# A fourth pair of k-tiles by seven block products in five of the eight chunks of an up projection

## The chip, the core and the metric

The kernel runs on one core of a Trainium2 chip. The core has a tensor engine (PE: matmuls and transposes, with a separate lane PEld that loads weights), a vector engine (DVE), a scalar engine (ACT), a general engine (POOL, here almost only an issuer of transfers) and a synchronisation engine (SP, which issues most transfers). Each takes its instructions in order from a queue of its own; they meet at semaphores. The metric is the device time of one execution in microseconds (us). Before the change it is 1054.91 us, the median of 3 runs (1053.62 to 1054.93).

## The reference, cut to what matters

One decoder layer in float32 on 256 positions of width 2048. Only the last part is touched:

```python
h = _rmsnorm(x, norm_mlp_pre)               # (256, 2048)
u = jnp.square(jax.nn.relu(h @ w_up))       # w_up is (2048, 8192)
x = x + _rmsnorm(u @ w_down, norm_mlp_post)
```

## The kernel before

**Precision.** Each float32 operand is split into a `hi` part, rounded to the format of the matmul, and a `lo` part, what is left. ACT makes `hi` with a copy, DVE makes `lo` with a subtraction (`split`, L288 to L292). A product is then three matmuls into the same bank: hi by hi, hi by lo, lo by hi (`three`). Where a weight row carries the gain of the norm, both engines apply it on the way (`split_gain`, L294 to L297; the DVE instruction is then a SCALAR_TENSOR_TENSOR).

**Tiles of the up projection.** The 8192 columns are cut into eight chunks of 1024 (`j`, 0 to 7), the 2048 rows into sixteen k-tiles of 128. The activations lie transposed in `hT` as hi and lo. A plain k-tile step ("k") loads one 128 x 1024 piece of `w_up` into a raw buffer through SP's queue, splits it, and runs 2 blocks of positions x 2 halves of columns x 3 = 12 matmuls of 512 columns into four accumulators.

**Seven products.** A step "w" takes two k-tiles together as a 2 x 2 by 2 x 2 block product and makes it from seven block products instead of eight. On the weights, DVE makes three sums (L343, L347, L348: two tiles `t` and `u`), and four tiles are split: the first block `b11` of 512 columns and the second row `b` from the buffer `ab`, then `u` and `t`. On the activations four "left sums" are made once per pair (`left_sums`) and kept in `st`; the pair's k-tiles of `hT` are overwritten with gain applied. Of the seven products three go to the accumulators and four to banks `m`; at the end of the chunk `close` combines the `m` into `c` on ACT and DVE, and four adds of DVE (L880) bring them to the accumulators. Seven times three are 21 matmuls. Before the change, chunks 1 to 7 have three such pairs (k-tiles 0 to 5) and ten plain k-tiles, in the order k-tiles 6 to 10, pair 0, 11, 12, pair 1, 13, pair 2, 14, 15 (`UP_STEPS`). Both k-tiles of a pair go through POOL's queue into one buffer `ab` of 2048 columns; in chunk 7 pairs 1 and 2 use two raw buffers instead.

**End of a chunk.** For each of its four accumulators (`up_evac`): the add on DVE, relu with the norm's scale on ACT (`r`, L883), four 128 x 128 transposes on PE (`rt`, L285) into the same bank, and the square on ACT into `uT` (L895). That work stands among the next chunk's first k-tiles. The bank is then free, and the next chunk's `m` are put into these four banks.

**What sets the order.** Every queue's order is written out by the program itself. `Weights` holds the list of tile splits and emits them `W_AHEAD` = 6 tiles ahead of the matmul that is being emitted; eight `hi` and eight `lo` buffers go round, so a split may run on the chip when PE is done with the tile eight before it. Sums of a pair are emitted two tiles ahead of its first split, but not before the end of the pair in front. `Flow` keeps a clock of its own, fed with a fixed cost per matmul, and inserts the evacuation chains when their delays have passed; `finish` forces what is left of a chain to be emitted at once. Raw buffers are five (`RAW_BUFS`).

## Time and profile before

| | before |
|---|---|
| three timed runs, median | 1054.91 us |
| profiled execution, its own time | 1055.26 us |
| span of the profiled execution, first to last instruction | 1053.5 us |
| PE busy in the span | 1042.6 us, 99% |
| DVE busy in the span | 819.8 us, 78% |
| ACT busy in the span | 622.5 us, 59% |
| mean granted clock of the tensor engine | 0.997 |

How to read it: "busy" is the time in which an engine worked on at least one instruction, as a share of the span. Lines of a timeline give the start in us from the span's start, the duration, engine, source line, operation, what it writes and reads, and in brackets the idle time of the engine ahead of it with what ended that. Matmuls overlap in the pipeline: the duration shown is that of one, while the distance between starts is what a row of them costs. In the windows, "(x200)" is a count of instructions, and PEclk the granted clock as a share of full speed. The first transposes of chunks 2 to 7 start at 451.38, 494.78, 538.18, 581.58, 624.98 and 668.38 us; "first transpose" always means the set of four 128 x 128 transposes of the first accumulator.

### The profile page before, as it was taken

The page shows a single profiled execution, that of the slowest core. Times are in us where ns is not written, and L with a number is a line of the kernel's source. Part 1 is how long each engine was busy: PE and PEld are TensorE (multiplying, and loading weights), DVE is VectorE, ACT ScalarE, POOL GpSimd, SP SyncE. Part 2 cuts the span into 40 slices and gives each one's busy share as a digit, 9 for nine tenths or more (in the row PEclk, how much of TensorE's full clock was granted, in tenths as well). Part 3 has the DMA queues.
Part 4 walks back from the last instruction along what each step waited for, and adds up shares of the span by engine and source line. Part 5 has one row for each costly group of instructions (what it writes and reads, how often), then busy time and mean ns, then how long its engine had stood idle before and what let it go on. Part 6 is the DMA issues. An engine that isn't in the chain of part 4 may idle for free.

```text
span 1053.5 us, 13402 instructions
## 1 busy us (share of the span) xinstructions
PE 1042.6 (99%) x4863; PEld 869.2 (83%) x4863; DVE 819.8 (78%) x1090; ACT 622.5 (59%) x832; POOL 46.7 (4%) x88
## 2 busy tenths in 40 slices
PE   9999999999999999999999999999999999999996
PEld 6888889888888788888888888888888888888885
DVE  6676536567557679879888888887899988998985
ACT  6584536565545467666665666666566665666661
POOL 0000000000000000010000100000000000000000
PEclk9999999999999999999999999999999999999998
DMA  9975447454447295647656466467466564667732
GB/s 299 355 236 145 144 130 241 143 161 158 141 167 234 79 350 167 222 143 237 197 186 201 160 215 207 148 224 238 162 218 206 195 221 148 224 210 253 262 121 80
DMA packets 74306, 206.26 MB, mean 196 GB/s; under 512 B 6912, under 2 KB 11520, under 8 KB 73856
## 3 DMA queue, kind: packets, MB, share of 16 engines
q1 hardware_dynamic: 63584, 168.06, 49.0%
q0 software_dynamic: 10080, 36.70, 9.7%
q8 instruction: 38, 0.62, 0.2%
q10 hardware_dynamic: 576, 0.64, 0.2%
q14 instruction: 28, 0.23, 0.1%
HBM read 201.18 MB, written 4.19 MB: 195 GB/s over the span
## 4 chain that ended last, share of the span: by engine, by line
PE 97%; DVE 1%; issue 1%; DMA 0%; ACT 0%; POOL 0%; DVEq 0%; POOLq 0%; ACTq 0%
PE y L281 27%; PE acc_u L281 25%; PE acc_o L281 8%; PE m L281 5%; PE md L281 4%; PE acc_qk L281 4%; PE acc_v L281 4%; PE acc_ckv L281 2%; PE acc_ukv L281 2%; PE acc_q L281 2%; PE acc_cq L281 2%; PE acc_k L281 2%; PE acc_uq L281 2%; PE rt L285 1%; PE sc_b L281 1%
## 5 line engine op out<-in xcount | busy, mean ns | idle before, releaser
L292 DVE TENSOR_TENSOR lo<-raw,hi 128x1024 fp32r<-128x1024 f32 (+3 forms) x219 | 249.2, 1153 | 93.8 <-ACT hi L291 93.1
L291 ACT ACTIVATE hi<-raw 128x1024 fp32r<-128x1024 f32 (+3 forms) x219 | 215.9, 1001 | 117.1 <-PE y L281 40.0
L281 PE MATMUL y<-hi,uhi 128*128 128x512 f32 x394 | 153.6, 390 | 0.0
L281 PE MATMUL y<-hi,ulo 128*128 128x512 f32 x394 | 153.3, 389 | 0.0
L281 PE MATMUL y<-lo,uhi 128*128 128x512 f32 x394 | 153.3, 389 | 0.0
L281 PE MATMUL acc_u<-hi,hT_hi 128*128 128x512 f32 x386 | 153.2, 397 | 0.0
L281 PE MATMUL acc_u<-hi,hT_lo 128*128 128x512 f32 x386 | 150.9, 391 | 0.4 <-DVE hT_lo L292 0.4
L281 PE MATMUL acc_u<-lo,hT_hi 128*128 128x512 f32 x386 | 150.6, 390 | 0.0
L296 DVE SCALAR_TENSOR_TENSOR lo<-raw,gcol,hi 128x1024 fp32r<-128x1024 f32 x86 | 107.6, 1278 | 12.5 <-ACT hi L295 12.3
L295 ACT ACTIVATE hi<-raw,gcol 128x1024 fp32r<-128x1024 f32 x86 | 97.9, 1151 | 24.2 <-PE acc_u L281 13.6
L281 PEld LDWEIGHTS y<-hi,uhi 128*128 128x128 f32 x394 | 74.0, 188 | 15.3
L281 PEld LDWEIGHTS y<-lo,uhi 128*128 128x128 f32 x394 | 74.0, 188 | 15.3
L281 PEld LDWEIGHTS y<-hi,ulo 128*128 128x128 f32 x394 | 73.9, 188 | 15.3
L281 PEld LDWEIGHTS acc_u<-hi,hT_lo 128*128 128x128 f32 x386 | 72.4, 188 | 16.2 <-DVE hT_lo L292 0.8
L281 PEld LDWEIGHTS acc_u<-lo,hT_hi 128*128 128x128 f32 x386 | 72.6, 188 | 14.2
L281 PEld LDWEIGHTS acc_u<-hi,hT_hi 128*128 128x128 f32 x386 | 72.6, 188 | 14.0
L281 PE MATMUL acc_o<-hi,mixT_hi 128*128 128x512 f32 x128 | 51.8, 405 | 0.0
L281 PE MATMUL acc_o<-hi,mixT_lo 128*128 128x512 f32 x128 | 50.2, 392 | 0.0
L281 PE MATMUL acc_o<-lo,mixT_hi 128*128 128x512 f32 x128 | 50.0, 390 | 0.0
L291 ACT ACTIVATE hi<-ab 128x512 fp32r<-128x512 f32 (+1 forms) x38 | 32.0, 843 | 30.0 <-PE acc_u L281 23.2
L281 PE MATMUL m<-hi,st 128*128 128x512 f32 x126 | 45.6, 389 | 0.0
L292 DVE TENSOR_TENSOR lo<-st_down,hi 128x1024 fp32r<-128x1024 f32 x34 | 40.9, 1218 | 2.7 <-ACT hi L291 2.7
(309 smaller groups left out, 1947.7 us busy)
## 6 DMA issues: line engine op xcount, KB each, us to landing
raw<-in_w_down SPq DMA_DIRECT2D x94, 512.0 KB, 4.7
raw<-in_w_up SPq DMA_DIRECT2D x86, 512.0 KB, 4.5
raw<-in_w_in SPq DMA_DIRECT2D x55, 512.0 KB, 5.0
ab<-in_w_up POOLq DMA_DIRECT2D x36, 512.0 KB, 4.9
ab_down<-in_w_down POOLq DMA_DIRECT2D x34, 512.0 KB, 6.2
raw<-in_w_out SPq DMA_DIRECT2D x32, 512.0 KB, 4.0
raw<-in_w_in SPq DMA_DIRECT2D x16, 288.0 KB, 2.8
raw<-in_w_ukv SPq DMA_DIRECT2D x8, 512.0 KB, 4.8
```

Of the source, the lines that this page charges most:

```text
L281: nc.tensor.matmul(out, a, b, start=start, stop=stop)
L285: nc.tensor.transpose(out, a, ident)
L291: nc.scalar.activation(hi, src, AF.Copy)
L292: nc.vector.tensor_tensor(out=lo, in0=src, in1=hi.bitcast(F32), op=OP.subtract)
L295: nc.scalar.activation(hi, src, AF.Copy, scale=g)
L296: nc.vector.scalar_tensor_tensor(out=lo, in0=src, scalar=g, in1=hi.bitcast(F32), op0=OP.mult, op1=OP.subtract)
```

## The change

Chunks 2 to 6 get a fourth pair (k-tiles 6 and 7), so they have four pairs and eight plain k-tiles, in the order k-tiles 8 to 11, pair 0, 12, pair 1, 13, pair 2, 14, pair 3, 15. Chunks 1 and 7 stay at three pairs. The fourth left sums are made during chunk 1, once its k-tiles 6 and 7 have been used plainly. From chunk 2 on, k-tiles 6 and 7 of `hT` carry the gain, so chunk 7 loads them without it. A second buffer `ab2` is used in turn with `ab`, and pair 2 of chunk 6 goes through two raw buffers. To make room, `st` keeps only three of the four left sums for pairs 0 to 2; the fourth (s1) is written into the block of `hT` that the seven products don't read; and two of the `uT` tiles lie in `ab2`. In a chunk with four pairs the last pair runs its products into `m` ahead of the others. Before the first pair of a chunk the evacuation chains of the previous one are finished.

```diff
-N_SEVEN, SUMS_AHEAD = 3, 2
-UP_STEPS = [("k", k) for k in range(6, 11)]
-for _i, _n in enumerate(((11, 12), (13,), (14, 15))):
-    UP_STEPS += [("w", _i)] + [("k", k) for k in _n]
+SUMS_AHEAD = 2
+
+
+UP_PAIRS = [()] + [("ab", "ab2", "ab", "ab2")] * 5 + [("ab2", "ab", "raw", "ab"), ("ab", "raw", "raw")]
+
+
+def up_steps(first, *groups):
+    steps = [("k", k) for k in first]
+    for i, ks in enumerate(groups):
+        steps += [("w", i)] + [("k", k) for k in ks]
+    return steps
+
+
+THREE = up_steps(range(6, 11), (11, 12), (13,), (14, 15))
+FOUR = up_steps(range(8, 12), (12,), (13,), (14,), (15,))
+UP_STEPS = [up_steps(range(16)), THREE] + [FOUR] * 5 + [THREE]
+
+ST = 13 * 256
+N_SEVEN = [sum(w == "w" for w, _ in steps) for steps in UP_STEPS]
...
-            if j == FF // CW - 1 and kp:
+            if UP_PAIRS[j][kp] == "raw":
                 return [weights.load(up_weight(j, 2 * kp + i), CW, f"raw_w{j}_{kp}{i}") for i in range(2)]
-            return load_two(late["ab"], nc.gpsimd if (j, kp) > (1, 0) else nc.sync,
+            return load_two(late[UP_PAIRS[j][kp]], nc.gpsimd if (j, kp) > (1, 0) else nc.sync,
...
-        for what, k in [("k", k) for k in range(KD)] if j == 0 else UP_STEPS:
+        for what, k in UP_STEPS[j]:
             if what == "k":
-                ts = [weights.plan(up_weight(j, k), 1, CW, gcol[:, 8 + k:9 + k])]
+
+                ts = [weights.plan(up_weight(j, k), 1, CW, *([gcol[:, 8 + k:9 + k]] if j < 2 or k >= 2 * max(N_SEVEN) else []))]
...
-            if j in (12, 13):
-                t2 = late["ab"][:, (j - 12) * CW:(j - 11) * CW]
+            if j in (10, 11, 12, 13):
+                t2 = late["ab2" if j < 12 else "ab"][:, j % 2 * CW:(j % 2 + 1) * CW]
...
-        four_sums(q, f)
-        st = [late["st"][:, i * 512:(i + 1) * 512] for i in (2 * kp, 2 * kp + 1)]
+        fs, qs = [x.rearrange("p (k s) -> p k s", s=P) for x in (f, q)]
+        keep = kp >= min(N_SEVEN[1:])
+        n = 512 if keep else 384
+        tt(out=qs[:, 0], in0=fs[:, 0], in1=fs[:, 1], op=OP.subtract)
+        tt(out=qs[:, 3] if keep else fs[:, 1], in0=fs[:, 1], in1=fs[:, 3], op=OP.subtract)
+        tt(out=qs[:, 1], in0=qs[:, 0], in1=fs[:, 3], op=OP.add)
+        tt(out=qs[:, 2], in0=fs[:, 2], in1=qs[:, 1], op=OP.subtract)
+        st = [late["st"][:, 768 * kp + i * n:768 * kp + (i + 1) * n] for i in range(2)]
         yield 3.0
-        for t, x in ((hs, f), (st, q)):
+        for t, x in ((hs, f), (st, q[:, :n])):
             nc.scalar.activation(t[0], x, AF.Copy)
         yield 1.5
-        for t, x in ((hs, f), (st, q)):
+        for t, x in ((hs, f), (st, q[:, :n])):
             tt(out=t[1], in0=x, in1=t[0].bitcast(F32), op=OP.subtract)
-        sums.append([[t[:, i * P:(i + 1) * P] for t in st] for i in range(4)])
+        s3, s2, s4, *s1 = [[t[:, i * P:(i + 1) * P] for t in st] for i in range(n // P)]
+        sums.append((s3, s1[0] if keep else [t[:, P:S] for t in hs], s2, s4))
         yield 0.5
 
     def all_sums():
-        for kp in range(N_SEVEN - 1):
+        for kp in range(2):
             yield from left_sums(kp)
         yield 8.0
-        yield from left_sums(N_SEVEN - 1)
+        yield from left_sums(2)
...
-    def seven_products(ts, left, accs, m, first, last):
+    def seven_products(ts, left, accs, m, first, last, m_first=False):
 
         (a11, a12, a22), (s3, s1, s2, s4) = left
         prods = ((a11, 0, 0, 1), (a12, 1, 0, (0, 0)), (s4, 1, 1, (0, 1)), (s2, 2, 0, 6), (a22, 2, 1, (1, 0)),
                  (s3, 3, 1, 7), (s1, 3, 0, 5))
+        if m_first:
+            prods = sorted(prods, key=lambda x: not isinstance(x[3], int))
         for p, (a, i, half, to) in enumerate(prods):
             w = weights.get(ts[i])
             in_m = isinstance(to, int)
             three(m[to] if in_m else accs[to], a, [w[x][:, half * 512:half * 512 + 512] for x in range(2)],
                   in_m and first, in_m and last)
-            if p == 6 or prods[p + 1][1] != i:
+            if all(x[1] != i for x in prods[p + 1:]):
...
-                late["st"] = late["up"].tile([P, 3 * CW], F32R, tag="st", bufs=1, name="st")
-                late["ab"] = late["up"].tile([P, 2 * CW], F32, name="ab")
+                late["st"] = late["up"].tile([P, ST], F32R, tag="st", bufs=1, name="st")
+                for n in ("ab", "ab2"):
+                    late[n] = late["up"].tile([P, 2 * CW], F32, name=n)
...
+            if (j, what, k, b) == (1, "k", 8, 0):
+                fourth = flow.start(left_sums(3), 20.0)
+            if j == 2 and t == 0:
+                flow.finish(fourth)
...
-            first, last = k == 0, k == N_SEVEN - 1
+            first, last = k == 0, k == N_SEVEN[j] - 1
             if first:
+                flow.finish(*evac[-4:])
                 m = {n: bank(i, f"m{n}_{j}") for n, i in zip((1, 6, 7, 5), free)}
             blocks = [[tok(hT[x], 2 * k + kk, bb) for x in range(2)] for kk, bb in ((0, 0), (1, 0), (1, 1))]
-            seven_products(tiles, (blocks, sums[k]), accs, m, first, last)
+            seven_products(tiles, (blocks, sums[k]), accs, m, first, last, last and N_SEVEN[j] > 3)
```

In `THREE` and `FOUR` the first argument lists the k-tiles ahead of pair 0, the others those behind each pair. `keep` is true for the fourth pair alone: its four sums all stay in `st`.

**The order at three places.** On DVE at the start of chunk 3, around the adds that evacuate chunk 2 (`acc_u_00` to `acc_u_11` are the four accumulators, `t_0`, `u_0` the sums of pair 0, `t_1`, `u_1` those of pair 1). Before:

```order
L292 TENSOR_TENSOR lo_4402<-ab,hi_4401 128x512
L292 TENSOR_TENSOR lo_4422<-ab,hi_4421 128x1024
L880 TENSOR_TENSOR acc_u_00_4050<-acc_u_00_4050,c_2_4374 128x512
L292 TENSOR_TENSOR lo_4439<-u_0_4358,hi_4438 128x1024
L880 TENSOR_TENSOR acc_u_01_4051<-acc_u_01_4051,c_2_4375 128x512
L880 TENSOR_TENSOR acc_u_10_4052<-acc_u_10_4052,c_2_4376 128x512
L292 TENSOR_TENSOR lo_4468<-t_0_4357,hi_4467 128x1024
L880 TENSOR_TENSOR acc_u_11_4053<-acc_u_11_4053,c_2_4377 128x512
L343 TENSOR_TENSOR t_1_4495<-ab 128x1024
L347 TENSOR_TENSOR u_1_4496<-t_1_4495,ab 128x512
```

Now:

```order
L896 TENSOR_TENSOR acc_u_00_4065<-acc_u_00_4065,c_2_4411 128x512
L307 TENSOR_TENSOR lo_4462<-t_0_4376,hi_4461 128x1024
L896 TENSOR_TENSOR acc_u_01_4066<-acc_u_01_4066,c_2_4412 128x512
L896 TENSOR_TENSOR acc_u_10_4067<-acc_u_10_4067,c_2_4413 128x512
L358 TENSOR_TENSOR t_1_4492<-ab_3502 128x1024
L362 TENSOR_TENSOR u_1_4493<-t_1_4492,ab_3502 128x512
L363 TENSOR_TENSOR u_1_4493<-u_1_4493,ab_3502 128x512
L311 SCALAR_TENSOR_TENSOR lo_4500<-raw_4497,gcol,hi_4499 128x1024
L896 TENSOR_TENSOR acc_u_11_4068<-acc_u_11_4068,c_2_4414 128x512
L307 TENSOR_TENSOR lo_4526<-ab_3502,hi_4525 128x512
L307 TENSOR_TENSOR lo_4560<-ab_3502,hi_4559 128x1024
```

The split of `t` has moved ahead of the second add, the sums of pair 1 and a k-tile ahead of the fourth add, and the two `ab` splits of pair 1 follow right behind that add.

On ACT and PE, at the transposes of the same chunk (`rt_0` are those of the first block of positions, `rt_1` of the second; `r` is relu, `uT` the square, `hi` the first half of a split). ACT before:

```order
L895 ACTIVATE uT_4485<-rt_0_4480 128x4x128
L883 ACTIVATE r_1_4487<-acc_u_10_4052,rstd_pre_3438 128x512
L295 ACTIVATE hi_4502<-raw_4500,gcol 128x1024
L883 ACTIVATE r_1_4512<-acc_u_11_4053,rstd_pre_3438 128x512
L895 ACTIVATE uT_4464<-rt_1_4514 128x4x128
L295 ACTIVATE hi_4528<-raw_4526,gcol 128x1024
L895 ACTIVATE uT_4485<-rt_1_4535 128x4x128
L291 ACTIVATE hi_4554<-ab 128x512
L291 ACTIVATE hi_4561<-ab 128x1024
```

ACT now:

```order
L911 ACTIVATE uT_4487<-rt_0_4482 128x4x128
L310 ACTIVATE hi_4499<-raw_4497,gcol 128x1024
L911 ACTIVATE uT_4517<-rt_0_4512 128x4x128
L899 ACTIVATE r_1_4519<-acc_u_10_4067,rstd_pre_3438 128x512
L306 ACTIVATE hi_4525<-ab_3502 128x512
L899 ACTIVATE r_1_4535<-acc_u_11_4068,rstd_pre_3438 128x512
L911 ACTIVATE uT_4487<-rt_1_4537 128x4x128
L911 ACTIVATE uT_4517<-rt_1_4549 128x4x128
L306 ACTIVATE hi_4559<-ab_3502 128x1024
```

The last two squares now stand next to each other, directly ahead of the `hi` of pair 1's second block; the first block of pair 1 stands ahead of the last relu. PE before, from the third transposes on:

```order
L285 MATMUL rt_1_4514<-ident,r_1_4487 128x128 x4
L281 MATMUL acc_u_10_4419<-hi_4364,hT_hi 128x512
L281 MATMUL acc_u_10_4419<-lo_4365,hT_hi 128x512
L281 MATMUL acc_u_10_4419<-hi_4364,hT_lo 128x512
L281 MATMUL acc_u_11_4420<-hi_4364,hT_hi 128x512
L281 MATMUL acc_u_11_4420<-lo_4365,hT_hi 128x512
L281 MATMUL acc_u_11_4420<-hi_4364,hT_lo 128x512
L281 MATMUL acc_u_00_4417<-hi_4385,hT_hi 128x512
L281 MATMUL acc_u_00_4417<-lo_4386,hT_hi 128x512
L281 MATMUL acc_u_00_4417<-hi_4385,hT_lo 128x512
L285 MATMUL rt_1_4535<-ident,r_1_4512 128x128 x4
L281 MATMUL acc_u_01_4418<-hi_4385,hT_hi 128x512
```

PE now:

```order
L300 MATMUL rt_1_4537<-ident,r_1_4519 128x128 x4
L296 MATMUL acc_u_10_4442<-hi_4389,hT_hi 128x512
L296 MATMUL acc_u_10_4442<-lo_4390,hT_hi 128x512
L296 MATMUL acc_u_10_4442<-hi_4389,hT_lo 128x512
L296 MATMUL acc_u_11_4443<-hi_4389,hT_hi 128x512
L296 MATMUL acc_u_11_4443<-lo_4390,hT_hi 128x512
L296 MATMUL acc_u_11_4443<-hi_4389,hT_lo 128x512
L300 MATMUL rt_1_4549<-ident,r_1_4535 128x128 x4
L296 MATMUL m_3_4555<-hi_4420,hT_hi 128x512
```

Six matmuls, not nine, lie between the third and the fourth transposes, and behind the fourth comes the first product of pair 0.

On DVE in chunk 1, in pair 2 (`u_2`; the plain k-tiles are the rows that read `raw` and `gcol`). Before:

```order
L292 TENSOR_TENSOR lo_3906<-u_2_3860,hi_3905 128x1024
L292 TENSOR_TENSOR lo_3916<-t_2_3859,hi_3915 128x1024
L296 SCALAR_TENSOR_TENSOR lo_3928<-raw_3925,gcol,hi_3927 128x1024
L296 SCALAR_TENSOR_TENSOR lo_3940<-raw_3937,gcol,hi_3939 128x1024
L296 SCALAR_TENSOR_TENSOR lo_3958<-raw_3955,gcol,hi_3957 128x1024
L296 SCALAR_TENSOR_TENSOR lo_3967<-raw_3964,gcol,hi_3966 128x1024
L296 SCALAR_TENSOR_TENSOR lo_3979<-raw_3976,gcol,hi_3978 128x1024
```

Now:

```order
L307 TENSOR_TENSOR lo_3910<-u_2_3864,hi_3909 128x1024
L949 TENSOR_TENSOR f_3919<-hT_hi,hT_lo 128x512
L951 TENSOR_SCALAR f_3919<-f_3919,gcol 128x256 x2
L955 TENSOR_TENSOR q_3920<-f_3919 128x128
L956 TENSOR_TENSOR q_3920<-f_3919 128x128
L957 TENSOR_TENSOR q_3920<-q_3920,f_3919 128x128
L958 TENSOR_TENSOR q_3920<-f_3919,q_3920 128x128
L307 TENSOR_TENSOR lo_3929<-t_2_3863,hi_3928 128x1024
L311 SCALAR_TENSOR_TENSOR lo_3941<-raw_3938,gcol,hi_3940 128x1024
L311 SCALAR_TENSOR_TENSOR lo_3953<-raw_3950,gcol,hi_3952 128x1024
L965 TENSOR_TENSOR hT_lo<-f_3919,hT_hi 128x512
L965 TENSOR_TENSOR st<-q_3920,st 128x512
```

The fourth left sums (`f`, `q`) stand between the splits of `u` and `t`, and the two subtractions into `hT_lo` and `st` behind the next two k-tiles.

More of the change, by code (lines that the diff above doesn't have):

```diff
@@ L1113, in layer @@
     dp = dpl["dp"] = pool("dp", "left")
-    late["st"] = up.tile([P, 3 * CW], F32, tag="st", bufs=1, name="st_down")
+    late["st"] = up.tile([P, ST], F32, tag="st", bufs=1, name="st_down")
     dpl["ab"] = dp.tile([P, 2 * CW], F32, name="ab_down")
```

## The prediction

> **What bounds the kernel now.** I read the page first, then the windows, then the three engines' timelines through one chunk of the up projection.
>
> ```profile
> span 1053.5 us, 13402 instructions
> PE 1042.6 (99%) x4863; PEld 869.2 (83%) x4863; DVE 819.8 (78%) x1090; ACT 622.5 (59%) x832; POOL 46.7 (4%) x88
> PE 97%; DVE 1%; issue 1%; DMA 0%; ACT 0%; POOL 0%; DVEq 0%; POOLq 0%; ACTq 0%
> ```
>
> PE is busy for 99% of the span and makes 97% of the chain that ended last, so a matmul removed is time removed, as long as PE finds its operands ready. Whether it will is not told by the 78% of DVE, which is an average over stages. The change acts on chunks 2 to 6, so I cut the trace from one first transpose of a chunk to the next, five equal stretches:
>
> ```profile
> core 0: us, PE busy (x) PEld busy (x) DVE busy (x) ACT busy (x) POOL busy (x), PEclk, DMA share, GB/s
> 494.78:538.17 43.39, 43.39 (x200) 35.92 (x199) 37.06 (x40) 27.25 (x31) 3.24 (x6) 1.00 0.59 194
> sum 216.97, PE 216.97 PEld 179.57 DVE 185.30 ACT 136.19 POOL 15.12; mean PE 43.39 PEld 35.91 DVE 37.06 ACT 27.24 POOL 3.02
> ```
>
> A chunk lasts 43.39 us and PE has no pause in it. DVE works 37.06 of them and has 6.33 to spare, at a granted clock of 1.00. That spare time is what the change spends.
>
> **What is removed.** A pair as two k-tiles costs 2 x 12 = 24 matmuls, as seven products 7 x 3 = 21. Five chunks each lose 3, in all 15; the order on PE has 15 rows fewer, so that the change might not do what it says is no rival here.
>
> ```profile
> 486.62 0.39 PE L281 MATMUL acc_u<-hi,hT_hi 128*128 128x512 f32 x1
> 494.78 0.60 PE L285 MATMUL rt<-ident,r 128*128 128x128 f32 x4
> 499.82 0.60 PE L285 MATMUL rt<-ident,r 128*128 128x128 f32 x4
> 502.34 0.60 PE L285 MATMUL rt<-ident,r 128*128 128x128 f32 x4
> ```
>
> From 486.62 to 494.78 are 36 matmuls, 0.2267 us each (the 0.39 shown is latency, not spacing). 15 x 0.2267 = 3.40 us. With nothing else, a chunk would last 43.39 - 0.68 = 42.71.
>
> **What is added on DVE.** Its spacing, start to start, is read where it runs without a gap:
>
> ```profile
> 507.29 1.22 DVE L292 TENSOR_TENSOR lo<-u,hi 128x1024 fp32r<-128x1024 f32 x1
> 508.43 1.22 DVE L292 TENSOR_TENSOR lo<-t,hi 128x1024 fp32r<-128x1024 f32 x1
> ...
> 526.32 1.22 DVE L343 TENSOR_TENSOR t<-ab 128x1024 f32<-128x1024 f32 x1
> 527.57 0.69 DVE L347 TENSOR_TENSOR u<-t,ab 128x512 f32<-128x512 f32 x1
> 528.30 0.69 DVE L348 TENSOR_TENSOR u<-u,ab 128x512 f32<-128x512 f32 x1
> 528.91 1.28 DVE L296 SCALAR_TENSOR_TENSOR lo<-raw,gcol,hi 128x1024 fp32r<-128x1024 f32 x1
> 530.10 2.27 DVE L977 TENSOR_TENSOR c<-m,c 128x512 f32<-128x512 f32 x3
> 532.41 0.69 DVE L977 TENSOR_TENSOR c<-c,m 128x512 f32<-128x512 f32 x1
> 533.02 1.28 DVE L296 SCALAR_TENSOR_TENSOR lo<-raw,gcol,hi 128x1024 fp32r<-128x1024 f32 x1
> 534.21 1.82 DVE L292 TENSOR_TENSOR lo<-ab,hi 128x512 fp32r<-128x512 f32 x2
> 535.95 0.69 DVE L880 TENSOR_TENSOR acc_u<-acc_u,c 128x512 f32<-128x512 f32 x1
> 536.55 1.21 DVE L292 TENSOR_TENSOR lo<-u,hi 128x1024 fp32r<-128x1024 f32 x1
> ```
>
> So: a split of 1024 columns 1.14; the sums of a pair 2.59 (526.32 to 528.91); a k-tile's split with gain 1.19; the four sums of `close` 2.92; the two splits from `ab` (512 and 1024 columns) 1.74; an evacuation add 0.60. A pair as seven products costs 2.59 + 1.74 + 2 x 1.14 = 6.61, as two k-tiles 2.38. Added: 4.23 per chunk. DVE then works 37.06 + 4.23 = 41.29 of 42.71 us: 1.4 us left. On the total it still fits; ACT gains about 1.3 on 27 and fits easily. The question is whether DVE can use every microsecond.
>
> **Where it can't: a loop through four queues.** In the changed order on ACT, the copies of the last two transposes stand directly before the `hi` split of pair 1's second block; before, a k-tile's split and the pair's first block stood around them. On PE the fourth transpose now comes after 6 matmuls and not 9, right before the first product of pair 0. So each chunk has this circle: fourth transpose (PE), its copy (ACT), `hi` of pair 1's second block (ACT), `lo` of it and everything queued behind it on DVE up to the first evacuation add of the next chunk, relu (ACT), first transpose (PE), and on to the fourth. Queued behind that `lo` is nearly all of DVE's chunk, and behind the add are relu and PE itself.
>
> ```profile
> 493.28 0.69 ACT L883 ACTIVATE r<-acc_u,rstd_pre 128x512 f32<-128x512 f32 x1 [2.63 <-DVE acc_u L880]
> ...
> 502.98 0.60 ACT L895 ACTIVATE uT<-rt 128x512 f32<-128x512 f32 x1 [0.71 <-PE rt L285]
> 503.47 0.62 ACT L291 ACTIVATE hi<-ab 128x512 fp32r<-128x512 f32 x1
> 505.05 1.06 ACT L291 ACTIVATE hi<-ab 128x1024 fp32r<-128x1024 f32 x1 [0.96 <-PE acc_u L281]
> ```
>
> ```profile
> 492.55 0.69 DVE L880 TENSOR_TENSOR acc_u<-acc_u,c 128x512 f32<-128x512 f32 x1
> 506.15 1.23 DVE L292 TENSOR_TENSOR lo<-ab,hi 128x1024 fp32r<-128x1024 f32 x1 [1.33 <-ACT hi L291]
> ```
>
> The steps of the loop:
> - Fourth transpose to `lo`: transposes 0.60, handover 0.04 (502.94 to 502.98), next on ACT after 0.49, `hi` 1.06, handover 0.04: 2.23. (In the new order nothing on PE holds the `hi`: the buffer that it takes was freed before pair 0.)
> - DVE from that `lo` to the add's end: the rest of pair 1, 3 x 1.14 = 3.42; sums, k-tile 13 and splits of pairs 2 and 3 with k-tile 14, 2 x (2.59 + 1.19 + 4.02) = 15.60; k-tiles 15, 8, 9: 3.57; the next chunk's first sums 2.59; k-tiles 10 and 11: 2.38; `close` 2.92; pair 0's `ab` splits 1.74 and `u` 1.14; the add 0.69. Sum 34.05.
> - Relu: handover 0.04 (the add of 492.55 ends at 493.24, the relu starts at 493.28) and 0.69: 0.73.
> - Relu to first transpose: no row of before shows PE waiting here. Bounds: 0.04, a bare handover, to 0.3, handover and the weight load of the transpose twice; I take 0.20, handover and one load, since PE can't load before relu is done.
>
> ```profile
> L285 PEld LDWEIGHTS rt<-ident,r x128: 138/140/143, 404.4 to 719.6; 128*128 128x128 f32 x128
> ```
>
> - First to fourth transpose: 494.78 to 499.82 is two stretches of nine matmuls, 5.04; the third with six, 2.52 - 0.68 = 1.84: 6.88.
>
> Loop: 2.23 + 34.05 + 0.73 + 0.20 + 6.88 = **44.09 us**. That is 0.70 more than the chunk of before and 1.38 more than PE needs: PE will pause about 1.4 us at the first transpose of each chunk. Five such intervals, from chunk 2's transpose to chunk 7's: 5 x 0.70 = +3.5 us; the 3.40 saved are inside that number. Bounds per loop: 43.8 (each handover and the transposes' end 0.3 less) to 44.5 (DVE waits on ACT once for 0.4). In chunk 7 the pause ends: it has three pairs, five k-tiles ahead of them, and the spare of before.
>
> The row 507.29 plus 1.22 ends after 508.43: DVE starts an instruction 0.08 before the one in front has ended. The Trainium skill (VectorE: DVE Perf Modes, "The DRAIN you can't avoid") says that the next one does not start until the pipeline is empty. By that rule the durations add up whole, the DVE part is about 1.8 longer per loop, and the sum would be 5 x 1.8 = 9 us higher, near 1068.5; the row speaks against it, and I use the spacing. What chance that rule has is counted with rival 3.
>
> **Chunk 1.** The fourth left sums are made here, on DVE, between the splits of pair 2:
>
> ```profile
> 405.25 0.68 DVE L932 TENSOR_TENSOR f<-hT_hi,hT_lo 128x512 f32<-128x512 f32 x1
> ...
> 407.61 1.22 DVE L292 TENSOR_TENSOR lo<-ab,hi 128x1024 fp32r<-128x1024 f32 x1
> ...
> 410.48 0.68 DVE L942 TENSOR_TENSOR hT_lo<-f,hT_hi 128x512 fp32r<-128x512 f32 x1
> ...
> 411.69 1.22 DVE L292 TENSOR_TENSOR lo<-t,hi 128x1024 fp32r<-128x1024 f32 x1
> ...
> 425.76 1.23 DVE L343 TENSOR_TENSOR t<-ab 128x1024 f32<-128x1024 f32 x1 [2.92 <-DMA ab<-in_w_up]
> ...
> 431.29 1.22 DVE L292 TENSOR_TENSOR lo<-u,hi 128x1024 fp32r<-128x1024 f32 x1
> ...
> 449.17 0.69 DVE L880 TENSOR_TENSOR acc_u<-acc_u,c 128x512 f32<-128x512 f32 x1
> ```
>
> ```profile
> 428.25 0.39 PE L281 MATMUL m<-hi,hT_hi 128*128 128x512 f32 x1
> ...
> 451.38 0.60 PE L285 MATMUL rt<-ident,r 128*128 128x128 f32 x4
> ```
>
> They cost 2.36 (405.25 to 407.61) plus 1.21 (410.48 to 411.69), and some 0.2 for four sums in place of three: 3.75. The second `ab` buffer takes away the wait of 2.92 at 425.76, but `lo<-u` needs a buffer that PE frees at 428.25 and a `hi` of 1.06, so it can start at 429.4, 1.9 earlier than at 431.29. The add moves from 449.17 to 451.0; + 0.69 + 0.73 + 0.20 puts the first transpose at 452.6, against 451.38: **+1.2 us**. Bounds: 0 (the sums fall into gaps) and 3.2 (the buffer gains nothing, or DVE and ACT hand over badly there).
>
> **Edits at nothing.** The smaller `st`, s1 in an unused block of h, u 10 and 11 in `ab2`: same work in another place, off PE; the copy into `ab2` stands behind its last split in ACT's order. Two k-tiles of chunk 7 without gain save 0.05 each on DVE, which has slack there. The pair through raw buffers in chunk 6 puts two loads on SP instead of POOL; the raw buffers they take were freed a pair earlier. If that cover is gone, a late load costs up to the 2.92 seen at 425.76, once. Running the last pair's products into m first lets `close` start earlier, but `close` comes late in DVE's queue, not for want of m.
>
> **Sum.** 3.5 + 1.2 = +4.7. The profiled execution took 1055.26 (span 1053.5 and 1.8 around it): 1059.96. The median of before is 0.35 lower: forecast **1059.6 us**.
>
> **The rivals.** A measurement of this kernel can tell about 0.2%, 2.1 us: faster is below 1052.8, slower above 1057.0.
> 1. PE stays the bound. Place: the first transpose; if the loop is at most 42.71, no pause, 5 x -0.68 = -3.4: 1051.5. For it: DVE's total of 41.29 fits. Against it: the loop would have to be 1.4 us shorter than its rows, with DVE's 34 us spaced as now. It decides from where ACT takes the `hi` of pair 1 without waiting for the last copy. Chance 0.13.
> 2. The loop comes out at 43.2 to 43.5 and chunk 1 hides its sums: about 0 to +1.5, 1055 to 1056.5. Chance 0.14.
> 3. DVE also waits for ACT inside its dense stretch. Before, `lo` waits for `hi` at several places, at 506.15 for over a microsecond; one such wait of 1.3 per chunk adds 6.5: about 1066. Against it: in that stretch a `hi` takes ACT 1.06 where its `lo` takes DVE 1.14, and ACT is idle for 16 us of a chunk. Chance 0.11.
>
> **How the numbers follow.** The forecast has 0.62, its own range 1057 to 1063.5 (2 to 8.7 more than 1054.9: 5 x 0.4 to 1.1, and chunk 1 at 0 to 3.2). Slower: 0.62 + 0.11 = 0.73; same 0.14; faster 0.13. The range for 8 in 10 leaves out rival 1 and most of rival 3, and takes in rival 2: 1054 to 1063.5.
>
> **What would show it.** PE idle until `rt`, 1 to 1.5 us, in chunks 2 to 7, with ACT r waiting for the DVE add before it; the first transposes 44.1 apart; DVE nearly without idle from pair 1 to the next add. I am wrong if PE has no idle before `rt` (rival 1), if the pauses are there but PE waits for `hi` or `lo` of a weight, or if the distance is under 43.4.

## The result and the profile after

| | before | after |
|---|---|---|
| median of the timed runs, taken together | 1054.92 us (1053.62 to 1055.11, 6 runs) | 1059.27 us (1057.91 to 1059.45, 6 runs) |
| ratio to before, 95% interval | | 1.004 (1.003 to 1.0051) |
| profiled execution, its own time | 1055.26 us | 1059.31 us |
| span | 1053.5 us | 1057.2 us |

Fifteen matmuls fewer, and 4.4 us more. The head of the page of the changed kernel and its chain of work that ended last:

```profile
span 1057.2 us, 13433 instructions
PE 1040.8 (98%) x4848; PEld 865.1 (82%) x4848; DVE 841.7 (80%) x1128; ACT 627.0 (59%) x844; POOL 50.9 (5%) x96
PE 88%; DVE 7%; issue 2%; ACT 1%; DMA 1%; POOL 0%; DVEq 0%; POOLq 0%; ACTq 0%
```

PE is busy 1.8 us less, the span is 3.7 us longer: PE now waits. In the chain DVE has 7% where it had 1%. The windows from one first transpose to the next, chunks 2 to 7 (columns as before: the stretch, its length, then busy time and count of each engine):

```profile
451.92:495.92 44.00, 43.08 (x197) 35.24 (x197) 40.88 (x45) 28.10 (x33) 4.31 (x8) 1.00 0.60 193
495.92:539.84 43.92, 43.00 (x197) 35.16 (x197) 40.79 (x45) 28.08 (x33) 4.32 (x8) 1.00 0.60 191
...
sum 219.74, PE 215.27 PEld 175.99 DVE 204.13 ACT 140.28 POOL 18.33; mean PE 43.05 PEld 35.20 DVE 40.83 ACT 28.06 POOL 3.67
```

A chunk has 3 matmuls fewer (197 records in place of 200) and lasts 43.95 us (219.74 / 5) in place of 43.39. DVE has 40.83 us of work in it, so it idles 3.1 us in every chunk although it is what PE waits for. Where PE waits, its timeline at the head of chunk 3 shows (start, duration, operation; in brackets the idle time ahead and what ended it):

```profile
490.36 0.39 PE L296 MATMUL acc_u<-hi,hT_lo 128*128 128x512 f32 x1
491.67 0.50 PE L296 MATMUL acc_u<-hi,hT_hi 128*128 128x512 f32 x1 [0.92 <-DVE c L1003]
...
495.92 0.60 PE L300 MATMUL rt<-ident,r 128*128 128x128 f32 x4
...
502.79 0.60 PE L300 MATMUL rt<-ident,r 128*128 128x128 f32 x4
```

From 490.36 to 491.67 are 1.31 us, 1.08 more than the spacing of 0.227. The pause is at the 7th matmul of the chunk, not at the first transpose. The waits of PE and of its weight loads in all the chunks (total, times, longest):

```profile
PEld acc_u L296 <- DVE c L1003: 7.6, 6, 1.4
PE acc_u L296 <- DVE c L1003: 5.1, 6, 1.0
PEld rt L300 <- ACT r L899: 1.5, 6, 0.3
```

DVE at the same place, and on to the split that starts its long run:

```profile
488.62 2.27 DVE L1003 TENSOR_TENSOR c<-m,c 128x512 f32<-128x512 f32 x3
490.93 0.69 DVE L1003 TENSOR_TENSOR c<-c,m 128x512 f32<-128x512 f32 x1
491.53 1.82 DVE L307 TENSOR_TENSOR lo<-ab,hi 128x512 fp32r<-128x512 f32 x2
493.27 1.22 DVE L307 TENSOR_TENSOR lo<-u,hi 128x1024 fp32r<-128x1024 f32 x1
494.40 0.69 DVE L896 TENSOR_TENSOR acc_u<-acc_u,c 128x512 f32<-128x512 f32 x1
...
505.00 1.23 DVE L307 TENSOR_TENSOR lo<-ab,hi 128x1024 fp32r<-128x1024 f32 x1 [2.61 <-ACT hi L306]
...
538.36 0.69 DVE L896 TENSOR_TENSOR acc_u<-acc_u,c 128x512 f32<-128x512 f32 x1
```

and ACT between the fourth transpose and that split, and at the next chunk's first relu:

```profile
503.42 0.60 ACT L911 ACTIVATE uT<-rt 128x512 f32<-128x512 f32 x1 [0.35 <-PE rt L300]
503.92 1.05 ACT L306 ACTIVATE hi<-ab 128x1024 fp32r<-128x1024 f32 x1
...
539.08 0.69 ACT L899 ACTIVATE r<-acc_u,rstd_pre 128x512 f32<-128x512 f32 x1 [4.58 <-DVE acc_u L896]
```

```profile
539.84 0.64 PE L300 MATMUL rt<-ident,r 128*128 128x128 f32 x4
```

These rows close the circle of the prediction, and their steps add up to its period of 43.92 us: the fourth transpose at 502.79, `hi` at 503.92, `lo` at 505.00, the add at 538.36, relu at 539.08, the first transpose at 539.84. DVE's 2.61 us of idle time ahead of `lo` is nearly all that it has in a chunk, and everything behind it in DVE's queue inherits the delay: the four closing sums (L1003), one of which lets PE's 7th matmul go, and the adds. The four banks `m` of a chunk are the banks into which the next chunk accumulates; the last closing sum (490.93, ending at 491.62) is the last reader of one of them, and PE goes on at 491.67. A second circle runs through that sum: its end to the 7th matmul 0.05, on to the first transpose 4.25 (495.92), to the fourth 6.87, to `lo` 2.21, and from `lo` to the end of the next last closing sum 30.57 (535.57; 534.88 and 0.69): 43.95.

### The profile page after: what moved, and what is told of

The parts are those of the page before. It is cut to its first block, busy times and chain, and to the rows that moved or that the text cites. A ratio compares the mean times of both kernels' runs of the same rounds, so it can differ in the third digit from the quotient of the medians.

```text
span 1057.2 us, 13433 instructions
## 1 busy us (share of the span) xinstructions
PE 1040.8 (98%) x4848; PEld 865.1 (82%) x4848; DVE 841.7 (80%) x1128; ACT 627.0 (59%) x844; POOL 50.9 (5%) x96
## 4 chain that ended last, share of the span: by engine, by line
PE 88%; DVE 7%; issue 2%; ACT 1%; DMA 1%; POOL 0%; DVEq 0%; POOLq 0%; ACTq 0%
PE y L296 26%; PE acc_u L296 18%; PE acc_o L296 8%; PE md L296 4%; PE acc_qk L296 4%; PE m L296 4%; PE acc_v L296 4%; PE acc_ckv L296 2%; DVE lo L311 2%; PE acc_ukv L296 2%; PE acc_q L296 2%; PE acc_cq L296 2%; PE acc_k L296 2%; DVE lo L307 2%; PE acc_uq L296 2%
## 5 line engine op out<-in xcount | busy, mean ns | idle before, releaser
L296 PE MATMUL acc_u<-hi,hT_hi 128*128 128x512 f32 x356 | 141.9, 399 | 5.1 <-DVE c L1003 5.1
L296 PE MATMUL acc_u<-hi,hT_lo 128*128 128x512 f32 x356 | 139.2, 391 | 0.4 <-DVE hT_lo L307 0.4
L296 PE MATMUL acc_u<-lo,hT_hi 128*128 128x512 f32 x356 | 138.8, 390 | 0.0
L311 DVE SCALAR_TENSOR_TENSOR lo<-raw,gcol,hi 128x1024 fp32r<-128x1024 f32 x74 | 93.1, 1279 | 9.3 <-ACT hi L310 9.1
L310 ACT ACTIVATE hi<-raw,gcol 128x1024 fp32r<-128x1024 f32 x74 | 83.3, 1146 | 21.7 <-PE acc_u L296 8.5
L296 PEld LDWEIGHTS acc_u<-hi,hT_hi 128*128 128x128 f32 x356 | 66.9, 188 | 20.4 <-DVE c L1003 7.6
L296 PEld LDWEIGHTS acc_u<-hi,hT_lo 128*128 128x128 f32 x356 | 66.8, 188 | 15.1 <-DVE hT_lo L307 0.9
L307 DVE TENSOR_TENSOR lo<-ab,hi 128x512 fp32r<-128x512 f32 (+1 forms) x46 | 42.5, 951 | 14.3 <-ACT hi L306 14.3
L899 ACT ACTIVATE r<-acc_u,rstd_pre 128x512 f32<-128x512 f32 x32 | 22.0, 687 | 41.4 <-DVE acc_u L896 40.5
L306 ACT ACTIVATE hi<-ab 128x512 fp32r<-128x512 f32 (+1 forms) x46 | 38.1, 842 | 11.9 <-PE acc_u L296 7.0
```

The costliest lines, as they stand in the source:

```text
L296: nc.tensor.matmul(out, a, b, start=start, stop=stop)
L306: nc.scalar.activation(hi, src, AF.Copy)
L307: nc.vector.tensor_tensor(out=lo, in0=src, in1=hi.bitcast(F32), op=OP.subtract)
L310: nc.scalar.activation(hi, src, AF.Copy, scale=g)
L311: nc.vector.scalar_tensor_tensor(out=lo, in0=src, scalar=g, in1=hi.bitcast(F32), op0=OP.mult, op1=OP.subtract)
L899: nc.scalar.activation(r, acc, AF.Relu, scale=rstd2[b])
```

## The experiments

The diffs show the lines that matter; helper lines around them are left out.

**1. The split ahead of the transposes' copies.** In the changed kernel, `hi` and `lo` of pair 1's second block are issued ahead of the last relu and squares of the chunk before:

```diff
                 w = weights.get(tiles[0])
+                if N_SEVEN[j] > 3 and steps[t + 1:] and steps[t + 1][:2] == ("w", 0):
+                    weights.emit(tiles[0] + 2 + weights.ahead)
```

> One split changes its place: in chunks 2 to 6 the hi and lo of pair 1's second block are emitted right behind those of its first block, so ahead of the last relu and of the last two squares on ACT, and no longer behind them. The work is the same. Loop theory (the circle fourth transpose, square, hi of pair 1's second block, the queue on DVE, close and first add, PE): the circle now starts at the next split, u, so it loses one DVE split of 1.14 us; 43.95 becomes 42.8 us per chunk, just above PE's own 42.71. 5 x -1.15 = -5.7 us: 1053.5 us, PE's waits for c nearly gone, faster than the kernel before. Load theory (a chunk lasts as long as DVE's total work and its unavoidable waits, wherever they stand): same work, 1059.3 us.

Measured: 1054.95 us (1053.47 to 1055.78, 11 runs), ratio to before 0.9999 (0.999 to 1.0008); 4.3 us of the loss are gone by moving one split, with all its work still there. Windows of this kernel between first transposes:

```profile
452.40:495.23 42.83, 42.83 (x198) 35.20 (x197) 40.84 (x45) 28.58 (x33) 4.30 (x8) 1.00 0.62 197
495.23:538.07 42.84, 42.84 (x198) 35.19 (x197) 40.83 (x45) 28.60 (x33) 4.30 (x8) 1.00 0.59 196
538.07:580.89 42.82, 42.82 (x198) 35.20 (x197) 40.83 (x45) 28.57 (x33) 4.30 (x8) 1.00 0.60 198
580.89:624.57 43.68, 43.05 (x198) 35.20 (x197) 40.93 (x45) 28.57 (x33) 3.21 (x6) 1.00 0.52 178
624.57:668.10 43.53, 43.11 (x198) 35.19 (x197) 40.84 (x46) 28.63 (x33) 2.15 (x4) 1.00 0.55 182
```

DVE works as long as in the changed kernel (40.83), and PE has no pause in three chunks. They last 0.12 more than the 42.71 of matmuls alone; the weight load of the 7th matmul still waits 0.20 for the closing sum there (at 491.01). So DVE's load was not too much: its place in the loop was. The last two intervals are 0.8 longer, which the expectation did not have, and so the time came out above the 1053.5 of the loop theory. On DVE a transfer is late there, chunk 6's first pair:

```profile
612.32 1.23 DVE L358 TENSOR_TENSOR t<-ab 128x1024 f32<-128x1024 f32 x1 [0.76 <-DMA ab<-in_w_up]
```

Chunk 5's last pair and chunk 6's first both use `ab2`, so this load can start only when the other's splits are done. Experiment 7 takes that up. In the second long interval no transfer is late; there PE waits 0.6 us for a closing sum (663.02 to 663.83 between two starts, less the spacing).

**2 and 3. The same work inside and beside the loop.** Two more sums of 512 columns on DVE in each of chunks 2 to 6. Inside: the first `u` sum of pair 2 is made three times (`again` is 2 there and 0 elsewhere). Beside: the same sum of pair 1, twice more, behind the `lo` of its first block, where DVE waits 2.61 us.

```diff
+            for _ in range(1 + again):
-            tt(out=u[:, :H], in0=t[:, :H], in1=b[:, H:], op=OP.add)
+                tt(out=u[:, :H], in0=t[:, :H], in1=b[:, H:], op=OP.add)
```

```diff
             if first:
+                if N_SEVEN[j] > 3:
+                    pt = pair_parts[sum(N_SEVEN[:j]) + 1]
+                    for _ in range(2):
+                        nc.vector.tensor_tensor(out=pt["u"][:, :512], in0=pt["t"][:, :512], in1=pt["b"][:, 512:], op=OP.add)
                 flow.finish(*evac[-4:])
```

> In chunks 2 to 6 one sum of pair 2 (512 columns) is computed three times instead of once, with the same result: 2 x 0.61 = 1.2 us of DVE per chunk, behind the lo of pair 1's second block, so inside the circle. Loop theory: each chunk longer by 1.2, 5 x 1.2 = +6.1 us on the changed kernel's 1059.3: 1065.4 us. Load theory: the same, 1065.4 us.

> The same two extra sums of 512 columns per chunk, but of pair 1 and placed directly behind the lo of its first block, where DVE waited 2.61 us for ACT: outside the circle. Loop theory: DVE's wait shrinks from 2.61 to 1.4 us and nothing else moves, 1059.3 us (within 0.5). Load theory: DVE has 1.2 us more work in every chunk, 1065.4 us as with the sums inside.

Beside: 1059.04 us (1057.65 to 1060.0), ratio 1.0039 (1.0025 to 1.0052), the changed kernel's own time. DVE's timeline of this kernel shows the additions eat the wait, with `lo` no later relative to what comes before it:

```profile
500.79 0.68 DVE L307 TENSOR_TENSOR lo<-ab,hi 128x512 fp32r<-128x512 f32 x1
501.38 1.41 DVE L1060 TENSOR_TENSOR u<-t,ab 128x512 f32<-128x512 f32 x2
504.07 1.23 DVE L307 TENSOR_TENSOR lo<-ab,hi 128x1024 fp32r<-128x1024 f32 x1 [1.27 <-ACT hi L306]
```

The theory that DVE's load as such sets the time falls with this. Inside: 1071.35 us (1070.41 to 1071.72), ratio 1.0155 (1.0141 to 1.0169), 12.1 us above the changed kernel where both theories gave 6. The sums account for 7.3: 1.46 per chunk (the group of three took 2.15 where one takes 0.69), five times:

```profile
511.84 2.15 DVE L363 TENSOR_TENSOR u<-t,ab 128x512 f32<-128x512 f32 x3
```

Another 3 us or so are the subject of the last section: PE's clock was halved twice after pauses. Of the rest, 0.7 stands in the profiled execution ahead of chunk 1's first transposes already (404.92 against 404.23), where no edit acts, and the median lies 0.9 above the profiled execution (1070.41). The place of chunk 1's first transposes differs like this from trace to trace, from 403.29 to 404.98; I don't know why.

**4. The side edits alone.** Three pairs in every chunk, all other edits kept (the second buffer, the smaller `st`, the fourth left sums still made in chunk 1, the forced evacuation):

```diff
-UP_STEPS = [up_steps(range(16)), THREE] + [FOUR] * 5 + [THREE]
+UP_STEPS = [up_steps(range(16))] + [THREE] * 7
...
-                ts = [weights.plan(up_weight(j, k), 1, CW, *([gcol[:, 8 + k:9 + k]] if j < 2 or k >= 2 * max(N_SEVEN) else []))]
+                ts = [weights.plan(up_weight(j, k), 1, CW, *([gcol[:, 8 + k:9 + k]] if j < 2 or k >= 8 else []))]
```

> All chunks 1 to 7 keep three pairs; the second buffer, the smaller st, the raw pair's place, the finished chains and the fourth left sums in chunk 1 stay (their result goes unused, but k-tiles 6 and 7 carry the gain from chunk 2 on). Loop theory: chunks are back at 43.4 us, and only chunk 1's sums show, as one pause at the start of chunk 2 of 0.5 to 1.2 us: 1055.4 to 1056.1 us. Rival (the added buffers and sums cost the time by themselves): most of the 4.3 us stays, 1058 to 1059 us.

Measured: 1055.78 us (1054.35 to 1056.44, 11 runs), ratio 1.0009 (1.0 to 1.0018). First transposes at 452.00 and 495.43, and from there on 43.38 to 43.40 apart; from chunk 1's (404.35) to chunk 2's it is 47.65, against 46.78 before the change. So the side edits cost 0.9 in chunk 1 and nothing per chunk. The per-chunk loss belongs to the fourth pair.

**5. The two ways out of DVE's queue.** PE paused at a place that the prediction did not name. Is the closing sum the true end of the loop, and the add and relu only near it? The last closing sum is formed from another bank, the same value, so that the 7th matmul's bank is read two sums earlier:

```diff
-                              (1, m[5], c[1], OP.add), (3, c[1], m[7], OP.subtract)):
+                              (1, m[5], c[1], OP.add), (3, m[5], c[2], OP.subtract)):
```

> The changed kernel, with the last of the four closing sums formed as m5 - c2 in place of c1 - m7 (the same value), so that the bank of m7, into which the 7th matmul of the next chunk goes, is free two sums (1.3 us) earlier, and the bank read last (m5) is the one of the 10th matmul. Two ways out of VectorE's queue nearly tie at the head of a chunk: the closing sum, after which the 7th matmul may go (the pause of 1.08 us at 491 us), and the add, relu and first transpose 4.2 us later. Theory A (both tie, so that opening one gives nothing): first transposes still 43.8 to 44.0 us apart, the pause shrinks at the 7th matmul and shows at the 10th and at the first transposes, time 1058.6 to 1059.6. Theory B (the closing sum alone sets the period): period down by up to 0.68 to 43.3, time 1055.8 to 1056.6.

Measured: 1058.54 us (1056.95 to 1059.58, 8 runs), ratio 1.0031 (1.002 to 1.0041). Windows and PE's timeline of this kernel:

```profile
452.09:495.93 43.84, 43.23 (x196) 35.20 (x196) 40.74 (x45) 28.09 (x33) 4.30 (x8) 1.00 0.59 192
495.93:539.78 43.85, 43.23 (x196) 35.20 (x197) 40.75 (x45) 28.10 (x33) 4.30 (x8) 1.00 0.59 193
```

```profile
495.93 0.44 PE L300 MATMUL rt<-ident,r 128*128 128x128 f32 x2 [0.51 <-ACT r L899]
```

The period stays at 43.84, as theory A had it, and now PE does stand before the first transpose, waiting for relu, in every chunk. So the loop of the prediction binds by itself once the other exit is open. In the changed kernel the circle through the closing sum, 43.95, is the longer one by 0.11: the closing sum stops PE just long enough, 4.2 us earlier, that it comes to the transpose when relu is ready.

**6. Only one pair of instructions exchanged on ACT.** The `hi` of pair 1's second block ahead of the last squares; `lo` and everything else stay in order on DVE.

```diff
             if first:
+                weights.get(tiles[0])
                 flow.finish(*evac[-4:])
```

> The changed kernel, with one pair of ScalarE's instructions exchanged at the head of each chunk: the hi of pair 1's second block is issued ahead of the last squares of the chunk before, its lo and all else stay in their order on VectorE. Loop theory: what VectorE's long run waits for comes 1 to 2 us earlier, so the period of 43.95 falls to between PE's own 42.8 and 43.3, time 1054.3 to 1056.2, with VectorE's wait for hi (2.61 us) down to 1.5 or less. Rival (VectorE's wait is only the slack that its load leaves, and the place of this hi does not matter): no change, 1058.8 to 1059.8.

Measured: 1056.47 us (1055.18 to 1057.82, 11 runs), ratio 1.0015 (1.0006 to 1.0024). Period 43.35 (first transposes from 452.71 to 669.46, five intervals); DVE's wait for `hi` fell from 2.61 to 1.66:

```profile
504.16 1.23 DVE L307 TENSOR_TENSOR lo<-ab,hi 128x1024 fp32r<-128x1024 f32 x1 [1.66 <-ACT hi L306]
```

The rival's "no change" falls, and the direction and about the size are the loop theory's; but period, time and wait lie 0.05, 0.3 and 0.16 above the top of what I had given. On ACT the `hi` (503.07) still follows the last relu (502.00) and a square (502.59), and chunk 2 began 0.8 later than in the changed kernel; 0.75 of that is there at chunk 1's first transposes (404.98 against 404.23), ahead of the edit.

**7 and 8. A version that beats both.** To experiment 1's edit is added, in `pairs_apart`, that from chunk 2 on no pair is loaded into the buffer that the pair just before it used (chunk 1's last pair and chunk 2's first still share `ab`); and in `all_three` besides this the closing sum of experiment 5 and an earlier start of the fourth left sums.

```diff
-UP_PAIRS = [()] + [("ab", "ab2", "ab", "ab2")] * 5 + [("ab2", "ab", "raw", "ab"), ("ab", "raw", "raw")]
+UP_PAIRS = [()] + [("ab", "ab2", "ab", "ab2")] * 4 + [("ab", "ab2", "ab", "raw"), ("ab2", "raw", "ab", "raw"), ("ab", "raw", "raw")]
...
-                fourth = flow.start(left_sums(3), 20.0)
+                fourth = flow.start(left_sums(3), 4.0)
```

> The kernel with the split moved ahead (hi and lo of pair 1's second block in front of the last relu), and besides no pair loaded into the buffer that the pair just before it used: chunk 5's last pair and two of chunk 6 go through the ring of the single rows. In that kernel the chunks of 42.8 us ended at chunk 5, where VectorE waited 0.76 us for a pair's transfer into a buffer used twice running, and the period was 43.7. Theory (that wait cost 0.85): 1053.8 to 1054.3. Rival (the ring of single rows runs short by the four more tiles it carries, and rows come late): 1055 or more.

> The same as the kernel with the pairs apart, with two more edits: the last closing sum as m5 - c2, and chunk 1's fourth left sums begun 16 us earlier, among VectorE's waits of 1.3 and 1.2 us at 418 and 428 us in place of its full stretch from 434 us. Theory (chunk 1's end and chunk 6's end each lose the pause at the 7th matmul, about 0.6 each): first transposes of chunk 2 at 451.2 to 451.7 in place of 452.4, time 1052.6 to 1053.4, faster than the kernel before by 0.15 to 0.2%. Rival (the left sums delay the first splits of chunk 1 by what they take, 3.4 us, and the closing sum only moves its pause to the next exit): 1054 or more.

`pairs_apart`: 1053.9 us, the median of eleven runs, ten of them from 1052.08 to 1054.24; ratio 0.9985 (0.9976 to 0.9994) without the eleventh. That one, the profiled execution, took 3748 us with its matmuls 0.84 us apart, for which I have no cause; so this version has no timeline that could be compared. In `all_three`, which has the same edit, DVE waits for no transfer in these chunks, and the interval that was 43.68 in experiment 1 is 42.71; two other edits came with it, so what this one gave by itself is not shown. `all_three`: **1051.88 us** (1051.28 to 1052.92, 7 runs), ratio 0.9972 (0.9961 to 0.9983), better than I had expected. Its windows:

```profile
450.19:492.90 42.71, 42.71 (x197) 35.28 (x196) 39.95 (x44) 28.48 (x33) 4.30 (x8) 1.00 0.59 191
492.90:535.62 42.72, 42.72 (x197) 35.28 (x197) 40.75 (x45) 28.58 (x33) 4.30 (x8) 1.00 0.60 197
...
578.31:621.02 42.71, 42.71 (x197) 35.33 (x197) 40.78 (x46) 28.55 (x33) 2.15 (x4) 1.00 0.54 182
621.02:664.36 43.34, 42.86 (x197) 35.22 (x197) 40.61 (x47) 28.64 (x33) 1.07 (x2) 1.00 0.55 183
```

Four chunks run at 42.71 us, which is the chunk of before less three matmuls to the hundredth, with DVE as busy as in the changed kernel. In the fifth, PE waits 0.48 for relu once more. The five intervals sum to 214.17 in place of 217.00 before the change, 2.8 less. Chunk 2's first transposes are at 450.19, 1.2 earlier than before the change, but that is no gain of these edits: chunk 1's are 1.2 earlier already (403.38 against 404.60), and from there to chunk 2's it is 46.81 against 46.78. How the gain divides among the three edits was not taken apart further.

**9. The fourth left sums early, alone.** The one number of the diff above, in the changed kernel.

> The changed kernel with one number changed: chunk 1's fourth left sums begin 16 us earlier, in a stretch in which VectorE waits 1.3 us twice for ScalarE, and no longer at 430 to 437 us, after which VectorE does not wait until chunk 1's end. Chunks 2 to 7 keep their loop. Theory (what the change costs in chunk 1 is that late work on VectorE): the first transposes of chunk 2 at 450.6 to 451.4 in place of 451.92, the five periods still 43.95, time lower by 0.5 to 1.3: 1057.9 to 1058.8. Rival (chunk 1's end is set by the splits and the closing sums, wherever the left sums stand): 451.7 or later, 1059.0 to 1059.6.

Measured: 1058.52 us (1057.59 to 1059.19, 5 runs), ratio 1.0035 (1.0023 to 1.0048). Chunk 2's first transposes came at 450.86, 1.06 earlier than in the changed kernel. Of this 0.15 is there at chunk 1's own (404.08 against 404.23); from those to chunk 2's it is 46.78 in place of 47.69, exactly as before the change. So where the left sums stood cost 0.9 us, all that chunk 1 had lost, and the rival falls. Of the five periods four are 43.83 to 43.96, as expected; the fourth is 44.46, and in it a transfer is late that was not late in the changed kernel's profile:

```profile
614.87 1.23 DVE L358 TENSOR_TENSOR t<-ab 128x1024 f32<-128x1024 f32 x1 [0.40 <-DMA ab<-in_w_up]
```

**10. The last pair's products in the usual order.** The prediction put "m first" among the edits at nothing.

```diff
-            seven_products(tiles, (blocks, sums[k]), accs, m, first, last, last and N_SEVEN[j] > 3)
+            seven_products(tiles, (blocks, sums[k]), accs, m, first, last)
```

> The changed kernel with the last pair's seven products in the order of the other pairs, in place of those first that go into the m banks. Prediction's theory (m and what it moves has slack, it lies under VectorE's queue): period 43.9 to 44.0 and time 1059.0 to 1059.6. Rival (since the closing sums, which read the m banks, release the next chunk's 7th matmul, they start later by up to four products of 0.68 us): period 44.5 or more, 1062 or more.

Measured: 1064.16 us (1063.0 to 1065.44, 5 runs), ratio 1.0087 (1.0073 to 1.0101): the prediction's theory falls here. DVE's timeline of this kernel at the head of chunk 3:

```profile
488.96 0.68 DVE L307 TENSOR_TENSOR lo<-ab,hi 128x512 fp32r<-128x512 f32 x1
489.56 2.27 DVE L1003 TENSOR_TENSOR c<-m,c 128x512 f32<-128x512 f32 x3
491.87 0.69 DVE L1003 TENSOR_TENSOR c<-c,m 128x512 f32<-128x512 f32 x1
492.47 1.22 DVE L307 TENSOR_TENSOR lo<-ab,hi 128x1024 fp32r<-128x1024 f32 x1
```

The closing sums do not wait for `m`, as the rival had it: DVE runs without a gap into them. But in the emitted order one split of pair 0, 0.60 us, now stands ahead of them. The period is 44.50, 0.55 more: the closing sum, and with it the pause of PE, is later by that split. That fits the circle through the closing sum (experiment 5), into which the split has moved. The rival's number came true by another mechanism, the place in DVE's queue. Between the first transposes of chunks 5 and 6 a wait of 0.81 for a transfer like that of experiment 1 comes on top, and PE's clock was halved (the interval is 47.03).

## Why the prediction was right, point by point

- **Matmuls removed, 3.40 us.** Right. The floor of 42.71 per chunk that follows from it is what the chunks of `all_three` last.
- **DVE's added work, 4.23 per chunk to 41.29.** Measured 40.83 busy, 3.77 more. Most of the 0.46 less is how busy time counts, by arithmetic on the rows: the 2.59 for a pair's sums holds 0.07 in which DVE is idle, and before the change DVE stopped four times more in a chunk (five idle times in brackets where now there is one); after a stop a split shows its full 1.22 and not 1.14, four times 0.08.
- **The loop, 44.09.** Right in its place and order. Step by step in the rows above: fourth transpose to `lo` 2.21 (2.23 predicted), `lo` to the add's end 34.05 (34.05), relu 0.72 (0.73), relu's end to the first transpose 0.07 (0.20), first to fourth transpose 6.87 (6.88); sum 43.92. That the sum meets the period is no test, since the rows follow one another around the circle; the test is that each step measures what was predicted from the rows of before. The term that was mis-sized is the one that had no row: a bare handover, the lower bound, would have been the better choice (0.07 here, 0.05 in experiment 5 where PE really waits there). Over five chunks the loop gave 219.74 - 217.00 = +2.7 in place of +3.5.
- **The place of the pause.** Wrong, and by a sign that the prediction itself named for being wrong: PE has no idle time before `rt`. I let PE pause at the first transpose, 1.4 us; it pauses 1.08 at the 7th matmul for a closing sum. The prediction followed DVE's queue to the add and did not ask what else in it PE waits for on the way: the banks `m` become accumulators again. Both ways out lie on the same run of DVE and nearly tie (43.95 through the closing sum, 43.84 through relu), so the period came out right all the same, and that they tie is luck; experiment 5 opens the one and finds the other.
- **Chunk 1, +1.2.** Measured +0.54 at chunk 2's first transposes (451.92 against 451.38), +0.9 counted from chunk 1's own, which were 0.4 earlier. The left sums took 3.38 on DVE and not 3.75, and the 0.13 of the handover counts here too. That they cost because they stand late in the queue is shown by experiment 9. The 0.4 by which chunk 1 itself began earlier is no effect of the change that any run shows.
- **The rest.** 2.7 + 0.5 = 3.3 at chunk 7's first transposes; the span is 3.7 longer. The missing 0.4 come later. Windows from 48 us after chunk 7's first transposes to the end, of the changed kernel and of the one before:

```profile
720.00:1057.20 337.20, 328.31 (x1453) 271.52 (x1451) 295.32 (x346) 194.12 (x221) 18.39 (x34) 0.99 0.57 193
```

```profile
716.72:1053.50 336.78, 328.30 (x1453) 271.49 (x1451) 295.17 (x346) 194.05 (x221) 18.39 (x34) 0.99 0.57 193
```

  PE's work is the same there and its pauses are 0.4 longer; no experiment looked at them. Adding the difference outside the span (2.1 against 1.8) the profiled executions differ by 4.05, the medians by 4.35: that the forecast of 4.7 is so close owes a little to luck, terms that were too large and others that were not counted.
- **Edits at nothing.** The side edits are worth nothing per chunk (experiment 4). "m first" is not: without it 4.9 us more are lost, of which 0.55 in each chunk is the loop's. And the second buffer has a price where two neighbouring pairs still share one: in the changed kernel's profile DVE waits for no transfer in these chunks, in three others it waits once for chunk 6's first pair, 0.76 (experiment 1), 0.40 (9) and 0.81 (10).
- **The rule of the Trainium skill (VectorE: DVE Perf Modes, "The DRAIN you can't avoid").** The 34.05 built from start-to-start spacing held to the hundredth, so the durations don't add up whole here. The prediction quoted only half of that section: it goes on that a next instruction that is not held starts earlier, and an earlier start is what the rows show (1.22 long, 1.14 apart).
- **The rivals.** PE as the bound (1) was not what happened, but its condition was named rightly: it decides from where ACT takes that `hi` without waiting for the last copy. Experiment 1 made just this, and PE had no pause in three chunks. DVE waiting in its dense stretch (3) did not occur.

## What to carry to other kernels

An engine with idle time left in every period can still set the period: look for the one wait in its queue behind which all its work stands, and follow the circle through every engine until it closes. Its idle time is free only on the near side of that wait (the same 1.4 us cost nothing there, and its full price and more behind it). When such a queue is late, list everything that others wait for along it, not just the first exit: opening one of two that nearly tie gave 0.1 us per chunk, while moving the head of the run, here one split ahead of two copies, gives it all back.

## What the runs showed of the hardware

PE's granted clock fell to half after two short pauses close together. PE in the kernel with the sums inside the loop, the head of chunk 4, and windows of it (the granted clock is the third number from the end):

```profile
536.93 0.50 PE L296 MATMUL acc_u<-hi,hT_hi 128*128 128x512 f32 x1 [0.74 <-DVE c L1005]
...
539.25 0.56 PE L296 MATMUL acc_u<-hi,hT_hi 128*128 128x512 f32 x1 [1.35 <-DVE c L1005]
539.60 0.63 PE L296 MATMUL acc_u<-lo,hT_hi 128*128 128x512 f32 x1
540.03 0.63 PE L296 MATMUL acc_u<-hi,hT_lo 128*128 128x512 f32 x1
```

```profile
540.00:543.00 3.00, 3.00 (x8) 2.34 (x7) 3.00 (x4) 0.29 (x1) 1.07 (x2) 0.51 0.54 160
543.00:548.00 5.00, 5.00 (x28) 4.11 (x26) 4.93 (x7) 2.73 (x4) 0.00 (x0) 1.00 0.32 115
```

Eight matmuls came 0.43 us apart in place of 0.227, some 1.5 us lost, twice in that run (chunks 4 and 6), which with the 7.3 of the sums gives about its 10.4 between first transposes of chunk 2 and 7. In the seven places of these runs with two such pauses (five here, two in experiment 10) it happened three times. The second pause had 1.34 or 1.35 of idle time in all seven, the first 0.74 to 0.77 where the clock fell and 0.29 to 0.73 where it did not, a difference too fine to call a threshold. Single pauses left the clock at 1.00: those of the changed kernel, about 1.1 us each, and also those in experiments 9 and 10 with the same 1.35 of idle time. The Trainium skill (TensorE: Matmul & The Clock Gate, "Why this matters for your kernels") warns of idle gaps of more than about 3 us. At these places no gap was longer than 1.5 us (1.35 of idle time and what the pipeline covers), though two fell within 3.4 us (from the last start ahead of the first pause, 535.81, to 539.25); what exactly decides was not tried.
